# Weight requests in ScalarE's queue, behind the copy of the unit four back

## The chip, the core and the metric

The kernel runs on one core of a Trainium2 chip. The metric is the device time of one execution in microseconds (us). The core has TensorE (matrix products), VectorE, ScalarE, GpSimd and SyncE; each works through its own list of instructions in order and waits for the others by semaphores. Transfers between HBM and the on-chip memory are asked for by an instruction in some engine's list, here almost all in SyncE's, and are then carried by 16 DMA engines.

## The reference

Two layers over 256 tokens of width 2048, all in float32, and a final RMSNorm:

```
layer 0: hn = rmsnorm(x); proj = hn @ w_in            (2048 x 6656)
         mixer A: 8 query heads on 2 key/value heads, band of +-128 tokens, ALiBi, a sink
         mixer B: 8 heads, three dilated windows merged by their softmax denominators, ALiBi
         x = x + (concat(A, B) * silu(z)) @ w_out     (2048 x 2048)
layer 1: hn = rmsnorm(x); q, k, v, z = hn @ w_in      (2048 x 8192)
         mixer C: 16 heads, 2-D neighbourhood attention with a relative bias
         x = x + (C * silu(z)) @ w_out                (2048 x 2048)
out    = rmsnorm(x) * g
```

The weights are 296 units of 512 KB; activations stay on chip.

## The kernel before

**Products.** A float32 product is made of three products of rounded parts: weight and activation are each split into a rounded high part and the rest. The list `PLAN` gives the blocks of columns in order. `block_fm` makes a block of 128 columns (2 units), `block_tm` one of 512 or 256 (8 or 4 units). Layer 1 ends its projections with four gate blocks of 512 columns (kind `"z"`), called z0 to z3 here.

**A weight unit's way.** `load_unit` (L132) keeps up to `AHEAD` = 5 units asked for: for each it takes one of five buffers `raw`, and asks for the unit in SyncE's list (L136). `split` (L146) rounds it on ScalarE into one of three buffers `wh` (L149, "the copy"), and VectorE forms what is left in one of three buffers `wl` (L150, "the rest"). TensorE then uses both parts (L172 and L174 in `block_fm`, L205 in `block_tm`). A buffer `raw` is free once copy and rest of its unit are done, so the request of a unit waits for the rest of the unit five before it. While the first block is made, each request is followed by one for the piece of x that goes with it (`load_x`, L507); later requests carry the four loads of x by rows (L606).

**Beside the weights.** Attention and gates run between the blocks, each piece some blocks later (`later`, `tick`), or one piece after each split (`chores`). A transpose of a 256 x 256 matrix is a *turn*: VectorE transposes 32 x 32 blocks (L249), SyncE stores them in HBM (L251), and four loads bring them back (L258). `gate` evacuates a gate block by four activations on ScalarE (L464, L465, two each) and two operations on VectorE (L466), and then turns it. Bias tables are loaded in SyncE's list too (L498, L503). So SyncE's one list holds weights, turns and tables.

**Order.** The code is written block by block, and a gate's evacuation stands in it before the splits of the next block. The framework that builds the program sets the order of each engine's list when it builds, so the lists follow the code only roughly; on the chip each list is strictly in order.

The functions that the change touches:

Of the kernel before, what the change touches and what calls it, by code (L numbers as in the profile page):

```python
# [32 lines left out]
AHEAD = 5  # L33
# [51 lines left out]
NU = sum(n * D // (P * UNIT) for _, _, _, n, _ in PLAN)  # L85
# [18 lines left out]
def build(tc, ctx, xt, xr_in, wt, head, sink, rpb, tabs, gl_in, out):  # L104
    nc = tc.nc
# [23 lines left out]
    pos = [0]  # L129
    beside, chores, ahead = deque(), deque(), deque()  # L130

    def load_unit():  # L132

        while len(ahead) < AHEAD and pos[0] < NU:
            raw = wp.tile([P, UNIT], F32, name="raw", bufs=AHEAD)
            nc.sync.dma_start(raw, wt[pos[0]])  # L136
            k = pos[0] * UNIT // PLAN[0][3]
            if k < NK:
                load_x(k, k + UNIT // PLAN[0][3])
            elif beside:  # L140
                beside.popleft()()
            pos[0] += 1
            ahead.append(raw)
        return ahead.popleft()

    def split(raw):  # L146
        h = wp.tile([P, UNIT], F32R, name="wh")
        lo = wp.tile([P, UNIT], F32R, name="wl")
        nc.scalar.copy(h, raw)  # L149
        nc.vector.tensor_sub(lo, raw, h.bitcast(F32))  # L150
        if chores:
            chores.popleft()()
        return h, lo
# [11 lines left out]
    def block_fm(aa):  # L165

        ps = ps_p.tile([P, 2, S], F32, name="pp")
        per = UNIT // HD
        parts = [split(load_unit()) for _ in range(NK // per)]
        ks = [(k, k // per, slice(k % per * HD, (k % per + 1) * HD)) for k in range(NK)]  # L170
        for k, u, c in ks[:-1]:
            nc.tensor.matmul(ps, parts[u][0][:, c], aa[:, k], start=k == 0, stop=False)  # L172
        for k, u, c in ks:
            nc.tensor.matmul(ps[:, 0], parts[u][1][:, c], aa[:, k, 0], start=False, stop=False)  # L174
        k, u, c = ks[-1]
        nc.tensor.matmul(ps, parts[u][0][:, c], aa[:, k], start=False, stop=True)  # L176
        return ps
# [7 lines left out]
    def block_tm(n, aa, begin=False):  # L185

        pss = [ps_p.tile([P, n], F32, name="pp") for _ in range(NT)]
        per = UNIT // n
        for u in range(NK // per):
            if not begin:  # L190
                h, lo = split(load_unit())
            elif u == 0:
                h, lo = first_unit(n)
            else:
                h, lo = split(load_unit())
                for k in range(u * per, (u + 1) * per):
                    split_x(k, 0, x[:, k, :])
            for kk in range(per):
                k = u * per + kk
                c = slice(kk * n, (kk + 1) * n)  # L200
                todo = [(t, i) for t in range(NT) for i in range(3)]
                if begin and u == 0:
                    todo.sort(key=lambda e: e[1])
                for t, i in todo:
                    nc.tensor.matmul(pss[t], aa[:, k, i // 2, t * P:(t + 1) * P], (h, lo, h)[i][:, c],  # L205
                                     start=k == 0 and i == 0, stop=k == NK - 1 and i == 2)
            if u % 2 and u < NK // per - 1:
                tick()
        return pss
# [296 lines left out]
    def load_x(k0, k1):  # L506
        nc.sync.dma_start(x[:, k0:k1, :], xt[:, k0:k1, :])  # L507
# [221 lines left out]
```

## Time and profile before

| | |
|---|---|
| time, median of 3 runs | 889.69 us (887.34 to 892.37) |
| the profiled execution | 889.07 us, its span 887.3 us |
| TensorE busy | 868.3 us, 98% |
| VectorE busy | 599.0 us, 68% |
| ScalarE busy | 502.4 us, 57% |
| HBM read and written | 187.7 and 21.0 MB, 235 GB/s over the span |
| share of TensorE in the chain of waits that ended last | 94% |

Times in the profile count from the start of the span. PE is TensorE's multiplication and PEld its load of stationary operands, DVE is VectorE, ACT ScalarE, SP SyncE, and SPq its list of requests. In a timeline a row has the start, the duration, the engine, the line, the operation, what it writes and reads, and how many were merged; in brackets stands how long the engine had been idle before it, and what ended that. An instruction in `[...] <-X` waited for X last.

### The profile page before, as it was taken

What the parts mean: (1) busy time and instruction counts of PE and PEld (TensorE: products, weight loads), DVE (VectorE), ACT (ScalarE), POOL (GpSimd) and SP (SyncE); (2) the same over time, 40 slices, a digit from 0 to 9 for tenths busy, and PEclk for the clock granted to TensorE, in tenths of its full rate; (3) what the DMA queues carried; (4) which work ended last, traced back from release to release, by engine and by line L of the source; (5) the groups of instructions that cost most, each with busy time, mean ns of one, the idle gap of its engine ahead of it and who ended that gap; (6) DMA issues with size and microseconds to landing.
All of it is one profiled execution on the core that took longest, in us unless ns stands there. A gap on an engine that the chain in (4) does not pass through costs nothing.

```text
span 887.3 us, 12303 instructions
## 1 busy us (share of the span) xinstructions
PE 868.3 (98%) x4218; PEld 732.9 (83%) x4218; DVE 599.0 (68%) x972; ACT 502.4 (57%) x858; POOL 0.9 (0%) x7
## 2 busy tenths in 40 slices
PE   9999999999999999999999999999999998899995
PEld 7898888889888888888888888888888876688884
DVE  6576867788677766667556666766666666666563
ACT  7646666676556555555455565556555655454452
POOL 0000000000000000000000000000000000000000
PEclk9999999999999999999999999999999999999999
DMA  9868777779767677777677767786687578667642
GB/s 353 305 201 256 223 248 254 214 228 278 225 211 233 230 239 252 245 240 241 214 238 233 258 223 259 226 268 243 200 272 272 196 220 297 197 208 274 210 165 96
DMA packets 104607, 209.53 MB, mean 236 GB/s; under 512 B 11744, under 2 KB 52704, under 8 KB 104416
## 3 DMA queue, kind: packets, MB, share of 16 engines
q1 hardware_dynamic: 104544, 208.74, 71.7%
q8 instruction: 33, 0.54, 0.3%
q14 instruction: 30, 0.25, 0.1%
HBM read 187.72 MB, written 20.97 MB: 235 GB/s over the span
## 4 chain that ended last, share of the span: by engine, by line
PE 94%; ACT 2%; DVE 1%; DMA 1%; issue 1%; SPq 0%; ACTq 0%; DVEq 0%
PE pp L205 70%; PE pp L172 10%; PE pp L174 6%; PE pp L293 1%; PE pp L292 1%; PE pp L294 1%; PE pS L369 1%; PE pY L163 1%; PE pY L162 1%; PE pS L368 1%; PE pS L367 1%; PE pY L161 1%; DMA raw<-wt 1%; DMA y<-xt 1%; PE pp L176 1%; ACT wh L149 1%
## 5 line engine op out<-in xcount | busy, mean ns | idle before, releaser
L150 DVE TENSOR_TENSOR wl<-raw,wh 128x1024 fp32r<-128x1024 f32 x291 | 354.5, 1222 | 218.7 <-ACT wh L149 188.8
L205 PE MATMUL pp<-wh,xx 128*128 128x512 f32 (+1 forms) x1472 | 457.1, 387 | 6.3 <-ACT wh L149 6.0
L149 ACT CAST wh<-raw 128x1024 fp32r<-128x1024 f32 x291 | 305.0, 1052 | 255.2 <-PE pp L205 207.1
L205 PEld LDWEIGHTS pp<-wh,xx 128*128 128x128 f32 x1472 | 275.8, 189 | 62.0 <-ACT wh L149 7.0
L205 PE MATMUL pp<-wl,xx 128*128 128x512 f32 (+1 forms) x736 | 285.3, 388 | 2.7 <-DVE wl L150 2.7
L205 PEld LDWEIGHTS pp<-wl,xx 128*128 128x128 f32 x736 | 139.4, 189 | 31.3 <-DVE wl L150 4.9
L205 PE MATMUL pp<-wh,yy 128*128 128x512 f32 x448 | 138.4, 389 | 0.0
L205 PEld LDWEIGHTS pp<-wh,yy 128*128 128x128 f32 x448 | 84.1, 188 | 17.5
L172 PE MATMUL pp<-xx,wh 128*128 128x512 f32 x390 | 93.7, 392 | 0.0
L205 PE MATMUL pp<-wl,yy 128*128 128x512 f32 x224 | 87.1, 389 | 0.0
L172 PEld LDWEIGHTS pp<-xx,wh 128*128 128x128 f32 x390 | 72.1, 188 | 14.6
L174 PEld LDWEIGHTS pp<-xx,wl 128*128 128x128 f32 x416 | 53.3, 191 | 2.0
L174 PE MATMUL pp<-xx,wl 128*128 128x256 f32 x416 | 54.0, 283 | 0.0
L205 PEld LDWEIGHTS pp<-wl,yy 128*128 128x128 f32 x224 | 42.1, 188 | 8.6
L379 ACT ACTIVATE s<-s,nm 128x256 f32<-128x256 f32 x64 | 32.0, 501 | 12.1 <-DVE nm L374 10.2
L371 DVE SCALAR_TENSOR_TENSOR s<-pS,qs,tab 128x256 f32<-128x256 f32 x64 | 28.4, 475 | 5.1 <-PE pS L369 5.0
L249 DVE STREAM_TRANSPOSE tt<-p 128x256 f32<-128x256 f32 x64 | 26.2, 435 | 7.9 <-ACT p L388 7.9
L388 ACT ACTIVATE p<-s,rd 128x256 f32<-128x256 f32 x64 | 29.0, 501 | 4.3 <-DVE rd L385 4.2
L181 ACT COPY sum<-pp 128x256 f32<-128x256 f32 x26 | 9.6, 371 | 37.5 <-PE pp L176 37.4
L407 ACT CAST ph<-pT 128x256 fp32r<-128x256 f32 x64 | 23.3, 405 | 11.3 <-DMA pT<-bounce 11.3
L408 DVE TENSOR_TENSOR pl<-pT,ph 128x256 fp32r<-128x256 f32 x64 | 24.4, 418 | 6.1 <-ACT ph L407 6.0
L374 DVE TENSOR_REDUCE nm<-s 128x2 f32<-128x512 f32 x32 | 21.7, 679 | 0.2
(124 smaller groups left out, 582.5 us busy)
## 6 DMA issues: line engine op xcount, KB each, us to landing
raw<-wt SPq DMA_DIRECT2D x295, 512.0 KB, 4.5
bounce<-tt SPq DMA_DIRECT2D x56, 256.0 KB, 2.7
pT<-bounce SPq DMA_DIRECT2D x224, 64.0 KB, 3.3
tab<-tabs SPq DMA_DIRECT2D x32, 128.0 KB, 4.9
tab<-rpb SPq DMA_DIRECT2D x16, 256.0 KB, 4.1
pair<-tt SPq DMA_DIRECT2D x16, 256.0 KB, 3.0
ka<-pair SPq DMA_DIRECT2D x64, 64.0 KB, 4.0
xr<-xr SPq DMA_DIRECT2D x4, 512.0 KB, 5.2
```

The costliest lines, as they stand in the source:

```text
L149: nc.scalar.copy(h, raw)
L150: nc.vector.tensor_sub(lo, raw, h.bitcast(F32))
L172: nc.tensor.matmul(ps, parts[u][0][:, c], aa[:, k], start=k == 0, stop=False)
L174: nc.tensor.matmul(ps[:, 0], parts[u][1][:, c], aa[:, k, 0], start=False, stop=False)
L205: nc.tensor.matmul(pss[t], aa[:, k, i // 2, t * P:(t + 1) * P], (h, lo, h)[i][:, c], start=k == 0 and i == 0, stop=k == NK - 1 and i == 2)
L249: nc.vector.transpose(tt[:, :, :, t, :].rearrange("p b c i -> p c b i"), srcs[t])
L371: nc.vector.scalar_tensor_tensor(s[:, t, :], pS[:, t, :], R["qs"][:, t:t + 1], tab[:, t, :], op0=OP.mult, op1=OP.add)
L374: nc.vector.tensor_reduce(nm, s, axis=AX.X, op=OP.max, negate=True)
L379: nc.scalar.activation(s[:, t, :], s[:, t, :], AF.Exp, bias=nm[:, t:t + 1], accum_out=den[:, t:t + 1])
L388: nc.scalar.activation(p[:, t, ::step], s[:, t, :], AF.Copy, scale=rd[:, t:t + 1])
L407: nc.scalar.copy(dh, src)
L408: nc.vector.tensor_sub(dl, src, dh.bitcast(F32))
```

## The change

The request of a unit moves from `load_unit` into `split`. `load_unit` only asks by itself when nothing has been asked for, which happens once, at the first unit after the head: then it asks for five units in SyncE's list as before. After that, `split` asks for one unit behind each copy, in ScalarE's list, so that four are ahead at any time. In this order the request of unit u + 4 stands behind the copy of unit u; its buffer is that of unit u - 1, whose rest must be done. The loads of x that go with the requests, the turns and the tables stay in SyncE's list.

```diff
-    def load_unit():
-
-        while len(ahead) < AHEAD and pos[0] < NU:
+    def fetch(n, eng):
+
+        while len(ahead) < n and pos[0] < NU:
             raw = wp.tile([P, UNIT], F32, name="raw", bufs=AHEAD)
-            nc.sync.dma_start(raw, wt[pos[0]])
+            eng.dma_start(raw, wt[pos[0]])
             k = pos[0] * UNIT // PLAN[0][3]
...
             pos[0] += 1
             ahead.append(raw)
+
+    def load_unit():
+        if not ahead:
+            fetch(AHEAD, nc.sync)
         return ahead.popleft()
 
     def split(raw):
...
         nc.scalar.copy(h, raw)
+        fetch(AHEAD - 1, nc.scalar)
         nc.vector.tensor_sub(lo, raw, h.bitcast(F32))
```

## Rows read from the trace of the kernel before

**Rows 1.** The page: busy time of each engine, share of the span, instructions.
```profile
PE 868.3 (98%) x4218; PEld 732.9 (83%) x4218; DVE 599.0 (68%) x972; ACT 502.4 (57%) x858; POOL 0.9 (0%) x7
```
**Rows 2.** Stretches: us; PE, PEld, DVE, ACT, POOL busy; clock; DMA share; GB/s.
```profile
0.00:10.00 10.00, 8.57 (x34) 7.24 (x35) 4.72 (x9) 5.47 (x8) 0.93 (x7) 1.00 0.78 274
10.00:12.00 2.00, 2.00 (x11) 1.62 (x10) 1.53 (x3) 1.84 (x4) 0.00 (x0) 1.00 1.04 416
10.00:704.00 694.00, 694.00 (x3464) 590.76 (x3463) 481.85 (x789) 406.63 (x709) 0.00 (x0) 1.00 0.75 245
...
740.00:744.00 4.00, 4.00 (x12) 3.16 (x11) 3.08 (x6) 0.86 (x1) 0.00 (x0) 0.57 0.99 330
764.00:768.00 4.00, 1.25 (x3) 0.80 (x4) 3.93 (x7) 4.00 (x7) 0.00 (x0) 0.91 0.17 66
768.00:772.00 4.00, 4.00 (x13) 3.12 (x12) 2.70 (x5) 0.75 (x2) 0.00 (x0) 0.66 0.79 243
```
**Rows 3.** Waits of TensorE in 704 to 736: total us, times, longest.
```profile
PE pp L205 <- DVE wl L150: 0.9, 3, 0.4
PE pp L205 <- ACT wh L149: 0.4, 1, 0.4
```
**Rows 4.** Timeline of TensorE, 704 to 780, its long waits.
```profile
737.58 0.73 PE L205 MATMUL pp<-wh,xx 128*128 128x512 f32 x2 [2.77 <-ACT wh L149]
739.16 0.50 PE L205 MATMUL pp<-wl,xx 128*128 128x512 f32 x1 [0.85 <-DVE wl L150]
...
765.88 0.73 PE L205 MATMUL pp<-wh,xx 128*128 128x512 f32 x2 [2.77 <-ACT wh L149]
767.48 0.80 PE L205 MATMUL pp<-wl,xx 128*128 128x512 f32 x1 [0.87 <-DVE wl L150]
```
**Rows 5.** Timeline of SyncE's list, 690 to 780.
```profile
708.87 0.34 SPq L251 DMA_DIRECT2D bounce<-tt  x1
...
712.60 0.38 SPq L136 DMA_DIRECT2D raw<-wt  x1
...
748.54 0.93 SPq L136 DMA_DIRECT2D raw<-wt  x2
```
**Rows 6.** Timeline of VectorE, 690 to 780: two of its rests.
```profile
700.11 1.23 DVE L150 TENSOR_TENSOR wl<-raw,wh 128x1024 fp32r<-128x1024 f32 x1 [1.50 <-ACT wh L149]
...
712.90 2.32 DVE L150 TENSOR_TENSOR wl<-raw,wh 128x1024 fp32r<-128x1024 f32 x2
```
**Rows 7.** Timeline of ScalarE, 690 to 780: copies and gates.
```profile
704.84 1.05 ACT L149 CAST wh<-raw 128x1024 fp32r<-128x1024 f32 x1 [2.05 <-PE pp L205]
...
706.88 0.69 ACT L464 ACTIVATE s<-pp,rh 128x512 f32<-128x512 f32 x1
...
755.84 1.04 ACT L149 CAST wh<-raw 128x1024 fp32r<-128x1024 f32 x1
...
762.47 0.69 ACT L464 ACTIVATE s<-pp,rh 128x512 f32<-128x512 f32 x1 [3.22 <-PE pp L205]
...
764.77 2.01 ACT L149 CAST wh<-raw 128x1024 fp32r<-128x1024 f32 x2
```
**Rows 8.** The tile raw, whole span: requests (ns), and time to landing.
```profile
L136 SPq DMA_DIRECT2D raw<-wt x295: 327/333/2128, 1.6 to 858.6; - x148
...
DMA to landing us min/median/max: 3.1/4.5/8.8
```
**Rows 9.** Waits of SyncE's list, whole span: total us, times, longest.
```profile
SPq L251 <- DVE tt L249: 111.2, 47, 8.3
...
SPq L136 <- DMA raw<-wt: 14.3, 14, 2.6
```
**Rows 10.** Timeline of ScalarE, 20 to 30: the copies of unit 7 and unit 10.
```profile
20.33 1.05 ACT L149 CAST wh<-raw 128x1024 fp32r<-128x1024 f32 x1 [0.86 <-PE pp L205]
...
28.49 1.05 ACT L149 CAST wh<-raw 128x1024 fp32r<-128x1024 f32 x1 [1.67 <-PE pp L205]
```
**Rows 11.** Groups of ScalarE: the copies, busy us, mean ns, idle before them.
```profile
L149 ACT CAST wh<-raw 128x1024 fp32r<-128x1024 f32 x291 | 305.0, 1052 | 255.2 <-PE pp L205 207.1 <-DMA raw<-wt 19.7 <-DMA pT<-bounce 7.6
```

## The prediction

> **What bounds the kernel now.** I began with the busy shares: the reader sees TensorE busy in 98% of the span, VectorE in 68%, ScalarE in 57% [rows 1]. So only time in which TensorE waits, or runs at a lower clock, can be won. The table of stretches shows where that is: from 10 to 704 us it is busy in every microsecond [rows 2], and beside the start and the last 9 us all of it lies between 704 and 772 us, in the gate blocks of layer 1 (z0 to z3, eight weight units each). There the waits of TensorE give 0.9 and 0.4 us in 704 to 736 [rows 3], and its timeline a pair at the start of z2, 2.77 us for the copy of the first unit and 0.85 for its rest (the difference that VectorE forms), and a second such pair at z3, 2.77 and 0.87 us [rows 4]. That is 7.26 us in four waits. [...] All in all 1.3 + 7.26 + 3.4 = 12.0 us are open to this change.
>
> Why these waits stand there is in SyncE's queue and in ScalarE's order. The rest of z0's last unit is done at 701.34 [rows 6], which frees the buffer of z1's unit 4; its request goes out only at 712.60, 11.3 us later, since SyncE stood before a turn whose transposes weren't done until 708.87, with more loads behind that [rows 5]. TensorE didn't need the unit yet, but the units of z1 come late one after another, and with them the 1.3 us. At z2 and z3 the order is what holds. z0's gate (706.88) has two copies for z1 ahead of it, the last at 704.84, so TensorE goes on while ScalarE evacuates; z2's gate starts at 762.47 with no copy for z3 ahead of it (the one at 755.84 is of z2's own last unit), and z3's first two copies come at 764.77, behind four activations [rows 7]. Yet those units were asked for at 748.54 [rows 5], and a unit lands within 8.8 us [rows 8], so they were there by 758.3. In the code every gate stands before the next block's copies, so each engine's list isn't the code's order: it was fixed when the program was built, by when the builder thought an operand would be there. With weights behind turns and loads in one queue it thought them late.
>
> **The change, part by part.**
>
> *Requests leave SyncE.* Of 295 requests [rows 8] the first five stay (the first fetch), 290 move. SyncE saves 290 x 0.33 = 96 us of issuing, which no chain needs: worth nothing by itself. What counts is that a weight no longer stands behind a turn that waits (111.2 us in 47 waits, the longest 8.3 [rows 9], hidden under TensorE everywhere but here), and a turn no longer behind a weight's buffer. In z1 to z3 the request comes right behind the copy of the unit four back, some 10 us before now. Four units take 4 x (1.05 + 1.67) = 10.9 us [rows 10], the landing 8.8 at most, so no copy waits for its weights. That takes the 1.3 us. Whether it also puts the first copies ahead of the gates of z1 and z2 hangs on the order in which the new program is built: bounds 0 and 7.26 + 3.4 = 10.7 us. I take the whole, by the nearest row, z0's gate, where they stand ahead and TensorE doesn't stop. What is late next there is VectorE's rest behind the gate, some 0.2 us by my estimate, as part of the 0.9 is [rows 3].
>
> *Requests enter ScalarE's queue.* No row shows a request in it. Below: nothing, since the copy before it runs 1.05 us and an issue takes 0.33. Above: SyncE's spacing in a burst, 0.93 us for two [rows 5], so 290 x 0.46 = 133 us. ScalarE idles 255.2 us just before the copies [rows 11], and in the steady stretch 1.67 us of each 2.72 [rows 10]; either end is covered there. Without cover, behind a gate with three copies in a row, it is 2 x 0.46 us on the third. I take 1.0 us for the whole run, between 0 and 3. [...]
>
> *A wait is added on ScalarE.* The request needs the rest of the unit before the one just copied. In the steady stretch that is done: copy and rest take some 2.3 us of 2.72. In z1's start it isn't: the rests of two units run from 712.90 to 715.22 [rows 6], after both copies, so a request behind the second copy holds ScalarE until the first is done at 714.1, at least 1.2 us, and behind it stand casts, softmax and the next copies. TensorE doesn't notice up to 3.1 us: copy and rest take 2.3 us, and the buffers they write are free two units, 5.44 us, before TensorE needs them. SyncE's requests also waited 14.3 us in 14 pieces, the longest 2.6, for an earlier transfer to land [rows 9]; that stays below 3.1. I take 0 here; what lies above it is the slow rival.
>
> *The start.* Unit 6 and later come through a second queue while the first still holds units 4 and 5 with their x. Asked for by 10 us (sizes from the code): 0.8 for the head, 5 x 0.52 for units, 5 x 0.26 for x, 4.7 MB; landed 274 GB/s x 10 = 2.7; the 2.0 left take 4.8 us at 416 GB/s [rows 2], or 9.6 if shared evenly with units 6 to 8. Then x of unit 5 lands at 19.6 and its split ends at 20.5, and TensorE begins unit 5 at 20.33, when the copy of unit 7 gets unit 4's buffer [rows 10]. Bounds 0 and 2 us, I take 0.5. The rows of x that SyncE may now load early (2 MB) stand behind these in its queue, so not before about 22 us.
>
> Sum, against the profiled execution (889.07 us, span 887.3 and 1.8 around it): -12.0 + 0.2 + 1.0 + 0.5 = -10.3, so 878.8. The median of the runs shown is 0.6 above that execution; I say 879.4.
>
> **The rivals.**
> R1, the order stays: the weights land early, but the gate's four activations still stand before the copies at z2 and z3. Then only the 1.3 us go, and 1.0 + 0.5 come: 889.3. For it: at z3 the weights were there and the order alone held TensorE. Against: the builder put them right at z0. Between lies that one of the two goes: 889.07 - 1.3 - 5.3 + 1.7 = 884.2.
>
> R2, the slower side: ScalarE is held at a request for over 3.1 us, in the stages with turns (30 to 320, 475 to 700), by a rest on VectorE that lags or by an earlier transfer which itself stands in SyncE behind a turn (up to 8.3 us [rows 9]); copies and evacuations behind it come late and TensorE runs dry. One such event costs what a pair costs, 3.6 + 1.7 = 5.3 us. With both z pairs gone it decides from the second event on; three give 878.8 + 16 = 894.8, and with the pairs still there a single one gives 889.3 + 5.3 = 894.6. For it: a queue in which nothing waited for a turn would be tied to one. Against: in 694 us there is no wait of TensorE at all now, so the slack is nowhere used up.
>
> R3, nothing moves: the transfers themselves are late, not their requests, since the same transfer engines carry both queues; then 889.1. For it: 416 GB/s at the start [rows 2], where they are all busy. Against: z3's first units were asked for 16 us before their copy. [...]
>
> **How the numbers follow.** Forecast (both pairs go) 0.42, with its own range of 877 to 882; one of the two goes 0.13; R1 0.17; R2 0.20; R3 0.08. Faster by over 0.5% (4.4 us, about what a measurement of this kernel tells from no change) means below 885.2: 0.55, the first two. Slower means above 894.1: 0.17 of R2's 0.20, as its mildest form ends below. Same: 0.28. The low end is all 12.0 us gone and nothing paid, 877.0; the high end is R2 in either form, 894.8, so 895.
>
> **What would show it.** Right: no wait of TensorE at the starts of z2 and z3, two copies ahead of each gate in ScalarE's timeline, a clock of 1.00 through 736 to 772, and ScalarE's requests some 10 us before the copies they serve. Wrong: copies still behind the gates (R1); waits of TensorE for copies inside 30 to 700 with a request ahead of them on ScalarE (R2); copies waiting for weights that were asked for in time (R3); or waits for x of over 2 us in all before 22 us.

## The result, and the profile after

The changed kernel takes 946.25 us (median of 6 runs, 944.90 to 955.89) against 889.34 before. The ratio of the means is 1.066, with a 95% interval of 1.061 to 1.071; one run of before, of 4205 us, is left out of it. The kernel is 57 us slower, where 879.4 and a range up to 895 were forecast.

The profiled execution of the changed kernel is its longest, 955.89 us with a span of 954.1 and a mean granted clock of 0.983, where the four shortest took 944.9 to 946.7 us at 0.992 to 0.994, so sums from its rows come out some 10 us too high. Its lines after L136 stand four to five lower than before: the copy is L153 (was L149), the rest L155 (L150), `block_tm` L210 (L205), a turn's store L256 and its loads L263 (L251, L258), the gate's activations L469 and L470 (L464, L465).

The page of after: busy shares, transfer queues, and the chain that ended last.

```profile
PE 898.6 (94%) x4218; PEld 736.2 (77%) x4218; DVE 595.4 (62%) x972; ACT 499.5 (52%) x858; POOL 0.9 (0%) x7
...
q10 hardware_dynamic: 41760, 152.06, 48.2%
q1 hardware_dynamic: 62784, 56.68, 19.3%
...
PE 62%; DMA 18%; DVE 9%; ACT 5%; SPq 3%; issue 2%; ACTq 0%; DVEq 0%
```

VectorE and ScalarE do what they did [rows 1]; TensorE's share falls from 98 to 94%. The weights' 152 MB now go through a queue of their own, q10. TensorE held 94% of the chain before; now transfers, VectorE and ScalarE make up a third of it. Of the 66.8 us by which the span grew, 36.5 are idle time of TensorE (954.1 - 898.6 less 887.3 - 868.3). The mean granted clock fell from 0.994 to 0.983 over the span; that is 10.9 us by estimate (0.017 x 954.1 less 0.006 x 887.3), and about what this execution took beyond the median, so the clock has next to no part in the 57 us. The other 19 are in longer busy time, the cause of which no view shows.

Stretches of after, with the columns of [rows 2]: the start, the stretch of layer 0 with turns, its end and the next projections, the attention of layer 1, and the rest.

```profile
0.00:100.00 100.00, 93.14 (x475) 78.32 (x476) 60.60 (x109) 56.46 (x100) 0.92 (x7) 0.98 0.70 243
100.00:320.00 220.00, 205.30 (x1081) 172.44 (x1080) 146.80 (x259) 121.03 (x238) 0.00 (x0) 0.98 0.67 209
320.00:475.00 155.00, 149.33 (x660) 119.53 (x659) 98.46 (x166) 76.99 (x119) 0.00 (x0) 0.99 0.68 220
475.00:704.00 229.00, 222.34 (x1011) 181.36 (x1010) 139.76 (x210) 120.51 (x205) 0.00 (x0) 0.99 0.73 236
704.00:954.10 250.10, 228.48 (x1000) 184.56 (x998) 149.81 (x233) 124.55 (x198) 0.00 (x0) 0.97 0.63 205
```

Where TensorE never stopped before (10 to 704 us [rows 2]) it now idles in every stretch. So the loss isn't at the gates z0 to z3 alone, on which the forecast was spent. The waits of TensorE over the whole span say for what (total us, times, longest), first before, then after:

```profile
PE pp L205 <- ACT wh L149: 6.0, 3, 2.8
PE pp L205 <- DVE wl L150: 2.7, 5, 0.9
...
PE pp L210 <- DVE wl L155: 29.5, 27, 3.8
PE pp L210 <- ACT wh L153: 5.0, 8, 1.0
PE pp L177 <- ACT wh L153: 3.7, 6, 1.2
```

It waits for split weights: 38.2 us for copies and rests, against 8.7 in all before. Yet the weights themselves are there. The views of ScalarE in after put 9.3 us, in 5 waits of its copies, down to a transfer of weights, where [rows 11] had 19.7 in all; and at four of the five the unit had landed over 5 us before its copy began, so that only the first, 1.17 us at 7.59, is a wait for weights. What stands ahead of the copies is shown by one place in ScalarE's timeline of after:

```profile
123.60 1.05 ACT L153 CAST wh<-raw 128x1024 fp32r<-128x1024 f32 x1 [0.96 <-DMA raw<-wt]
128.48 0.34 ACTq L136 DMA_DIRECT2D raw<-wt  x1
129.00 0.41 ACT L412 CAST ph<-pT 128x256 fp32r<-128x256 f32 x1 [4.35 <-DMA pT<-bounce]
...
129.62 2.00 ACT L153 CAST wh<-raw 128x1024 fp32r<-128x1024 f32 x2
```

and by the same place of before (the third pair of casts of turned softmax there, L407):

```profile
113.74 1.06 ACT L149 CAST wh<-raw 128x1024 fp32r<-128x1024 f32 x1 [0.87 <-PE pp L205]
114.72 0.71 ACT L407 CAST ph<-pT 128x256 fp32r<-128x256 f32 x2
```

Before, 39 copies stand ahead of this cast and it finds its operand there. After, only 37 do, and ScalarE idles 4.35 us until the turn has landed; two copies come behind it, and TensorE waits 0.39 us for the rest of the first (131.98). This place alone doesn't tell the cast from the request ahead of it, which went out only at 128.48; the experiments do. The chain of after from 98 to 132 us shows two turns in a row on the path that sets the end (start, us, what):

```profile
99.00 3.82 DMA bounce<-tt
...
104.40 5.02 DMA pT<-bounce
109.54 0.76 DVE y L488 x2
110.31 1.15 DVE wl L155
111.50 3.26 PE pp L210 x13
...
119.20 4.55 DMA bounce<-tt
...
125.10 3.83 DMA pT<-bounce
129.00 0.46 ACT ph L412 x2
129.62 1.05 ACT wh L153
130.70 1.24 DVE wl L155
131.98 5.29 PE pp L210 x22
```

From the start of its store to the end of its loads a turn takes some 10 us; an addition of VectorE or a cast of ScalarE waits for them, and a rest or copy for TensorE waits behind that.

The turns are slower, too. The pages of before (the first two lines) and after have, of transfers by line, KB each and the median us to landing:

```profile
bounce<-tt SPq DMA_DIRECT2D x56, 256.0 KB, 2.7
pT<-bounce SPq DMA_DIRECT2D x224, 64.0 KB, 3.3
...
raw<-wt ACTq DMA_DIRECT2D x290, 512.0 KB, 4.4
bounce<-tt SPq DMA_DIRECT2D x56, 256.0 KB, 4.2
pT<-bounce SPq DMA_DIRECT2D x224, 64.0 KB, 4.3
```

and the waits of SyncE's list, before and after, for its loads behind their store:

```profile
SPq L258 <- DMA bounce<-tt: 31.9, 36, 3.8
...
SPq L263 <- DMA bounce<-tt: 130.4, 45, 5.7
```

The lists themselves, compared instruction by instruction in the built programs (the shift is the mean over all places):

```
places that differ    ScalarE      VectorE      TensorE
after / before        611 of 768   812 of 970   1891 of 4205
mean shift            2.1          2.6          4.1 places
```

On ScalarE, what consumes a turn stands on average 1.4 copies earlier in after, and the activations of softmax 2.2.

### The profile page after: what moved, and what is told of

Read it like the earlier page. It is cut to its first block, busy times and chain, and to the rows that moved or that the text cites. A ratio compares the mean times of both kernels' runs of the same rounds, so it can differ in the third digit from the quotient of the medians.

```text
span 954.1 us, 12128 instructions
## 1 busy us (share of the span) xinstructions
PE 898.6 (94%) x4218; PEld 736.2 (77%) x4218; DVE 595.4 (62%) x972; ACT 499.5 (52%) x858; POOL 0.9 (0%) x7
## 4 chain that ended last, share of the span: by engine, by line
PE 62%; DMA 18%; DVE 9%; ACT 5%; SPq 3%; issue 2%; ACTq 0%; DVEq 0%
PE pp L210 45%; DMA pT<-bounce 8%; PE pp L177 6%; DMA bounce<-tt 5%; PE pp L179 4%; DVE wl L155 4%; SPq L263 2%; DMA raw<-wt 2%; ACT wh L153 2%; DVE tt L254 1%; DMA pair<-tt 1%; DVE s L376 1%; DVE s L471 1%; DMA ka<-pair 1%; DMA sk<-sink 1%
## 5 line engine op out<-in xcount | busy, mean ns | idle before, releaser
L210 PE MATMUL pp<-wh,xx 128*128 128x512 f32 (+1 forms) x1472 | 463.8, 393 | 7.3 <-ACT wh L153 4.7
L155 DVE TENSOR_TENSOR wl<-raw,wh 128x1024 fp32r<-128x1024 f32 x291 | 351.6, 1219 | 108.5 <-ACT wh L153 107.2
L153 ACT CAST wh<-raw 128x1024 fp32r<-128x1024 f32 x291 | 301.8, 1049 | 119.4 <-PE pp L210 73.0
L210 PEld LDWEIGHTS pp<-wh,xx 128*128 128x128 f32 x1472 | 277.0, 192 | 64.5 <-ACT wh L153 8.2
L210 PE MATMUL pp<-wl,xx 128*128 128x512 f32 (+1 forms) x736 | 292.6, 398 | 24.4 <-DVE wl L155 24.1
L210 PEld LDWEIGHTS pp<-wl,xx 128*128 128x128 f32 x736 | 141.4, 192 | 64.8 <-DVE wl L155 37.0
L210 PE MATMUL pp<-wh,yy 128*128 128x512 f32 x448 | 140.7, 393 | 0.4 <-ACT wh L153 0.3
L177 PE MATMUL pp<-xx,wh 128*128 128x512 f32 x390 | 97.2, 394 | 3.9 <-ACT wh L153 3.7
L210 PEld LDWEIGHTS pp<-wh,yy 128*128 128x128 f32 x448 | 84.6, 190 | 18.9 <-ACT wh L153 1.7
L210 PE MATMUL pp<-wl,yy 128*128 128x512 f32 x224 | 89.1, 398 | 5.5 <-DVE wl L155 5.4
L210 PEld LDWEIGHTS pp<-wl,yy 128*128 128x128 f32 x224 | 42.4, 189 | 18.7 <-DVE wl L155 10.1
L412 ACT CAST ph<-pT 128x256 fp32r<-128x256 f32 x64 | 23.1, 406 | 39.0 <-DMA pT<-bounce 27.1
L488 DVE TENSOR_TENSOR y<-y,pT 128x256 f32<-128x256 f32 x22 | 8.5, 422 | 29.0 <-DMA pT<-bounce 23.3
```

What stands on the lines that cost most here:

```text
L412: nc.scalar.copy(dh, src)
```

## The experiments

Theories: **hold** (R2: ScalarE stands at a request, and what is behind it is late), **order** (the builder laid other lists, and copies stand behind waits for turns), **rings** (weights in a second queue make the transfers of turns slower). Before took 889.3 to 889.5 us in each set of runs; intervals are of the ratio to it.

**1. Hold alone.** The bulk of each unit goes through SyncE again; the last 8 columns, 4 KB, are asked for by ScalarE at the changed place, behind the same buffers.

```diff
-            eng.dma_start(raw, wt[pos[0]])
+            if eng is nc.scalar:
+                nc.sync.dma_start(raw[:, :UNIT - 8], wt[pos[0]][:, :UNIT - 8])
+                nc.scalar.dma_start(raw[:, UNIT - 8:], wt[pos[0]][:, UNIT - 8:])
+            else:
+                nc.sync.dma_start(raw, wt[pos[0]])
```

> Weights go back to SyncE's list, all but the last 8 of 1024 columns of each unit (4 KB), which ScalarE asks for where the change put the whole request; so both lists keep a request per unit, and ScalarE's has the same waits as in the changed kernel. Theory order (the builder sees SyncE's list nearly empty, thinks turns quick, and lists their consumers ahead of the copies, which then wait for the turn): 885 to 900 us, as SyncE's list is as full as before. Theory rings (turns take longer because weights come through a second queue beside them): 885 to 900, as the weights are back in the turns' queue. Theory hold (ScalarE is held at its requests by VectorE's rests and by earlier transfers): 930 to 950.

Measured: 887.42 us, 0.998 [0.997, 0.999]. 290 requests on ScalarE, most of them with a wait, cost nothing. The lists of ScalarE, VectorE and TensorE differ from before's in 152, 197 and 156 places only, by 0.2 to 0.3 on average. The run speaks for short holds alone: in its timeline ScalarE stands idle until a request goes out for 79.6 us in all, never over 1.9 at once, while after has as much in all, 79.3 us, but twelve pieces beyond the start of 2 to 4 us.

**2. The mirror.** ScalarE asks for 1016 columns, SyncE for the last 8.

> The mirror of the run before: ScalarE asks for 1016 of 1024 columns of each unit, SyncE for the last 8 at the same place of the code. Theory order: 885 to 905, SyncE's list has a request for each unit again. Theory rings: 940 to 955, the bulk still comes through the second queue. Theory hold: 940 to 955, ScalarE waits for the same as in the changed kernel.

Measured: 945.18 us, 1.062 [1.059, 1.065], like after. I expected SyncE's list, full of requests again, to bring before's order back. It didn't: the lists differ in 609, 813 and 1833 places. Between these two kernels the order went with the long transfers, not with the number of requests. So this run does not tell order from rings; it only shows that the bytes, and not the number of requests in a queue, carry the loss.

**3. Another engine asks.** The same requests in GpSimd's list, which has nothing else to do.

```diff
-        fetch(AHEAD - 1, nc.scalar)
+        fetch(AHEAD - 1, nc.gpsimd)
```

> The requests of the change are made by GpSimd, which has nothing else to do, instead of ScalarE; SyncE's list is as empty as in the changed kernel. Theory hold: 880 to 900, as no engine with work is held. Theories order and rings: 935 to 955, since SyncE's list is empty and the weights come through a queue of their own.

Measured: 934.76 us (923.54 to 943.79), 1.047 [1.039, 1.054]. Here no request can hold ScalarE, and 41 us (by the ratio) to 45 (by the median) are still lost. What the rest of the 57 are isn't told by this run, nor does it put a price on the hold: its lists are others again (310, 364 and 127 places off before's, 627, 796 and 1919 off after's).

**4. Three ahead.** The request then needs the rest of the unit two before the copy, which is long done.

```diff
-        fetch(AHEAD - 1, nc.scalar)
+        fetch(AHEAD - 2, nc.scalar)
```

> The changed kernel with three units ahead instead of four in the same five buffers, so that a request behind a copy needs the rest of the unit two before, not one before. Theory hold, if it is the rests that hold ScalarE: below 925. Theories order and rings: 940 to 965, the lead of three units (8.2 us) is hardly more than the longest landing (8.3), so it may be worse than the change.

Measured: 954.62 us, 1.076 [1.071, 1.080]. A wait for VectorE's rest is not what costs: the waits of ScalarE that its view puts down to a rest fall from 43.9 us in after to 3.6, with lists that differ from after's in 4, 6 and 0 places, and nothing is gained.

**5. The new place alone.** The request behind the copy and four ahead, but in SyncE's list.

```diff
-        fetch(AHEAD - 1, nc.scalar)
+        fetch(AHEAD - 1, nc.sync)
```

> The requests stand where the change puts them, behind the copy of the unit four back, but in SyncE's list. Theories order and rings: 885 to 895, since it is the second queue that does the harm and not the place or the lead of four. If the lead of four were too short: 930 and more.

Measured: 889.11 us, 1.000 [0.999, 1.001]. ScalarE's, VectorE's and TensorE's lists are those of before, without a difference. So place and lead cost nothing; the queue does.

**6 and 7. Order and queue, each alone.** At the end of the build, every instruction of ScalarE, VectorE and TensorE (requests for transfers excepted) is tied behind the one that should precede it, by a dependency that orders the list and adds no semaphore. Before, tied to its own lists, builds into the same program, so the ties themselves change nothing. SyncE's list is left to the builder, and without the weights it is 231 and 224 of 431 places off before's in the two kernels, so each difference below has some of SyncE's order in it. One kernel is after with before's three lists, the other before with after's three lists.

```diff
         tick()
+    pin(tc)
...
+        for a, b in zip(seq, seq[1:]):
+            tc.add_manual_dep(b, a.name, info, reason="order")
```

> The changed kernel, weights asked for by ScalarE, but the lists of ScalarE, VectorE and TensorE (requests aside) are tied to the order that they have in the kernel before, by order-only dependencies that make nothing wait on the chip. Theory order (the lost time comes from lists in which consumers of turns stand earlier): 878 to 895 us. Theory rings (turns take longer on the chip beside the second queue): 930 to 950, as the weights still come through it. Theory hold is out already.

> The mirror: the kernel before, weights asked for by SyncE, with the three lists tied to the order of the changed kernel. Theory order: 925 to 960, or more, as turns stand behind weights again. Theory rings: 885 to 900.

Measured: 904.01 us, 1.016 [1.015, 1.018], for after with before's lists, and 927.21, 1.043 [1.039, 1.047], for before with after's lists. The four kernels make a table:

```
weights asked for in    before's lists   after's lists   by the lists
SyncE's queue           889.4            927.2           37.8
ScalarE's queue         904.0            946.3           42.3
by the queue            14.6             19.1
```

So two thirds of the loss or more go with the lists, whichever queue the weights are in; and with the weights in SyncE's queue no request stands in ScalarE's list to hold it. After's lists make TensorE wait for rests even with one queue. From the views of waits, TensorE in before with after's lists:

```profile
PE pp L205 <- DVE wl L150: 17.9, 21, 2.9
PE pp L205 <- ACT wh L149: 4.3, 4, 2.4
```

and in after with before's lists:

```profile
PE pp L210 <- ACT wh L153: 8.1, 4, 2.8
PE pp L210 <- DVE wl L155: 7.8, 7, 2.9
```

Of the 15.9 us in the latter, 7.25 are before's two pairs at z2 and z3 [rows 4]. Two more waits, 1.42 us at 301.28 and 2.34 at 316.03, follow casts at which ScalarE stands for a turn, with no request going out in between:

```profile
298.48 0.41 ACT L412 CAST ph<-pT 128x256 fp32r<-128x256 f32 x1 [4.24 <-DMA pT<-bounce]
...
312.35 0.41 ACT L412 CAST ph<-pT 128x256 fp32r<-128x256 f32 x1 [6.67 <-DMA pT<-bounce]
```

The waits of ScalarE and of SyncE's list over the whole span show the slow turns as well:

```profile
ACT ph L412 <- DMA pT<-bounce: 65.2, 24, 6.7
...
SPq L263 <- DMA bounce<-tt: 155.7, 47, 6.5
```

Its page has 4.1 us for a store and 4.4 for a load. Before, that cast waited 11.3 us in 7 pieces, and the loads 31.9 in 36. With after's lists and one queue, the page has 3.4 and 3.2.

**8 and 9. What slows the turns.** Both with before's lists. First, ScalarE asks for 1016 columns and SyncE for 8, so that SyncE's list keeps the pace of the weights; second, each unit comes by two requests of 512 columns, so its rows are half as long.

```diff
+                nc.scalar.dma_start(raw[:, :UNIT - 8], wt[pos[0]][:, :UNIT - 8])
+                nc.sync.dma_start(raw[:, UNIT - 8:], wt[pos[0]][:, UNIT - 8:])
...
+                eng.dma_start(raw[:, :UNIT // 2], wt[pos[0]][:, :UNIT // 2])
+                eng.dma_start(raw[:, UNIT // 2:], wt[pos[0]][:, UNIT // 2:])
```

> The lists of the kernel before, ScalarE asks for 1016 of 1024 columns of each unit and SyncE for the last 8. If the 15 us that stayed with the lists of before tied come from the weights' bytes in a second queue: 898 to 912. If they come from SyncE's list running ahead without requests that wait for buffers: 886 to 895.

> The lists of the kernel before, the whole weights asked for by ScalarE, each unit in two requests of 512 columns, so with rows of 2 KB instead of 4 KB. If turns lose on the transfer engines because their short rows take turns with the weights' long ones: pT<-bounce lands in under 4.0 us (4.4 with the long rows) and the time is 892 to 901. If not: 4.3 or more and 900 to 915.

Measured: 913.71 us, 1.027 [1.024, 1.031], and 917.33, 1.030 [1.028, 1.032]. The first says that SyncE's list running ahead of the weights isn't the cause, since tied to their pace again it loses more; a store takes 4.1 us and a load 4.0 there. The second is inconclusive: loads land in 3.8 us, stores in 4.3, and the time isn't lower, so the length of a weight's rows isn't shown to be what matters; its view of ScalarE also puts 50.8 us of waits of copies down to weights, where after with before's lists has 7.1. What goes on between two queues on the 16 transfer engines stays open, but the traces narrow it. A store that is asked for while no unit is under way (asked for and not yet landed) lands in 2.0 to 2.1 us (medians) in before, in after, and in after with before's lists; there are 17 such stores of 56 before, and 6 and 4 in the other two. Asked for beside one unit, a store takes 3.0, 4.0 and 3.8 us. So stores meet a weight more often, and land later beside one. In before with after's lists, in one queue, a store beside one unit takes 3.7 us, so landing later isn't the second queue's alone.

**10. Only where the gain was seen.** Requests in ScalarE's queue from z0 on, in SyncE's before that.

```diff
+        if pos[0] >= IZ:
+            fetch(AHEAD - 1, nc.scalar)
```

> ScalarE asks for weights only from the first unit of z0 on; all earlier ones are asked for by SyncE, five ahead, as in the kernel before. Forecast's reason (in the gate blocks SyncE's queue holds weights back): 877 to 886, the two pairs of waits gone. Theories order and rings: the part after 684 us, 23% of the time, loses like the whole, about 15 us, so 895 to 908.

Measured: 890.28 us, 1.002 [1.000, 1.003]. Waits of TensorE from 700 to 780 us in it:

```profile
PE pp L212 <- DVE wl L157: 6.7, 6, 2.7
PE pp L212 <- ACT wh L154: 0.8, 1, 0.8
```

The pairs of [rows 4] began with a wait for a copy, 2.77 us each; those are gone, but rests are late in their place. The builder's new order isn't the wanted one here either.

**11 and 12. The wanted order, written out.** Before with its own lists tied, but for this: the first two copies and rests of z2 and of z3 stand ahead of the gates of z1 and z2. Weights in SyncE's queue in one kernel, in ScalarE's from z0 on in the other.

> The kernel before, weights in SyncE's list, with its own lists tied except that the first two copies of z2 and of z3, and their rests, stand ahead of the gate of the block before. If the order alone holds the two pairs of waits: 877 to 883 us, 10.7 us less at most (7.3 of waits, 3.4 of clock). If the weights are too late there for lack of an early request: 886 to 895, the copies then keep the gate waiting.

> The same lists, and ScalarE asks for the weights from z0 on. If SyncE's queue held the weights back in the gate blocks: 874 to 882, below the run before by the 1.3 us of small waits and more. If the second queue costs there what it costs over the whole kernel (some 15 us in all, 3 to 4 in this quarter): 881 to 890, above the run before.

Measured: **877.80 us, 0.986 [0.984, 0.988]**, with every request in SyncE's list, in before's order: 1.4% faster than before, and the lowest time here. With ScalarE asking from z0 on, 880.60 us, 0.989 [0.987, 0.991], an interval that meets the other. Two stretches of the faster one, with the columns of [rows 2]:

```profile
736.00:744.00 8.00, 7.40 (x31) 5.84 (x32) 7.80 (x14) 5.73 (x13) 0.00 (x0) 1.00 0.82 263
764.00:772.00 8.00, 8.00 (x39) 6.73 (x39) 4.15 (x5) 3.43 (x4) 0.00 (x0) 1.00 1.00 309
```

ScalarE's timeline of it, before and at the gates of z1 and z2:

```profile
733.72 1.05 ACT L149 CAST wh<-raw 128x1024 fp32r<-128x1024 f32 x1 [0.26 <-DMA raw<-wt]
735.05 1.05 ACT L149 CAST wh<-raw 128x1024 fp32r<-128x1024 f32 x1 [0.28 <-PE pp L205]
736.00 0.68 ACT L464 ACTIVATE s<-pp,rh 128x512 f32<-128x512 f32 x1
...
756.58 1.06 ACT L149 CAST wh<-raw 128x1024 fp32r<-128x1024 f32 x1 [0.27 <-ACT wh L149]
758.58 0.69 ACT L464 ACTIVATE s<-pp,rh 128x512 f32<-128x512 f32 x1 [0.94 <-PE pp L205]
```

The waits of its TensorE for split weights, whole span:

```profile
PE pp L205 <- DVE wl L150: 2.1, 5, 0.5
...
PE pp L205 <- ACT wh L149: 0.2, 1, 0.2
```

Copies stand ahead of each gate, TensorE waits 2.3 us for split weights in the whole span, and the granted clock is 1.00 where it was 0.57 and 0.66 [rows 2].

## Why the prediction was wrong, point by point

**The step that failed** is in the part on leaving SyncE: the order in which the new program is built. It was priced at two places, as a gain between 0 and 10.7 us, and taken at the gain. The premise was right: lists are fixed when the program is built, by when the builder thinks an operand will be there. But the same premise holds for every list over the whole span. With weights in a queue of their own the lists were built with what consumes a turn 1.4 copies further ahead, and on the chip the turns don't come that early (its casts of turned softmax wait 27.1 us for loads in after, 11.3 before); that the builder thought they would is an inference. These lists cost 38 to 42 us, shown by exchanging them with the queue unchanged (6 and 7). "The order changes" had a rival in which it stays, and none in which it gets worse elsewhere.

**Rival R3 and the second queue.** The forecast gave a late transfer the price of nothing moving, 889.1, with a chance of 0.08; by it a second queue gains nothing and costs nothing. That both queues use the same transfer engines is in after's trace: of the time of 16 engines, q1 alone takes 101.9% from 8 to 9 us, q10 alone 94.8% from 53 to 54, and the two side by side 52.5 and 50.9% from 19.5 to 20.5. The profiles of these runs also bear out that the second queue brings no transfer forward (a unit lands in 4.4 us at the median, 4.5 before), but not that it costs nothing: with the three lists held fixed, the second queue takes 14.6 us on before's lists and 19.1 on after's, with stores of turns at 4.1 us for 2.7. That a turn might get slower was in no term of the sum. It is shown to come with the weights' bytes in the other queue (8); how, is shown only as far as stores meet a weight more often there.

**R2** had the right sign and a wrong mechanism. It asked for ScalarE held at a request for over 3.1 us. Before with after's lists has no request in ScalarE's list and loses 37.8 us (7); three units ahead, with hardly a wait for rests left, gains nothing (4). Holds aren't absent in after: of the twelve pieces of 2 to 4 us named in experiment 1, three are over 3.1. What these cost isn't separated; it is within the 14.6 to 19.1 us by the queue. Nor is every wait that is put down to a weight's transfer a hold: the view of ScalarE's waits puts 18.8 us, in five pieces, of instructions that read no weight (softmax, casts of turns and of heads, squares) down to a transfer of a weight, but in the timeline the last request ahead of each had gone out 2.9 to 4.6 us before. The remark against R2, that the slack is nowhere used up in 694 us, was true of before's lists alone, and a stretch without a wait doesn't tell how much slack is left.

**The term for issuing** (1.0 us, between 0 and 3) holds: 334 ns each at the median in the view of the tile raw, and 887.42 us in experiment 1, not above before. The lower bound is seen too: in after's timeline a request goes out at 30.56 us, while ScalarE's copy ahead of it runs from 30.50 to 31.55.

**The weights are there in time**: right. Units land in a median of 4.4 us, and of the five waits put down to a transfer only the 1.17 us of the first unit, which SyncE asks for, is a copy waiting for its own.

**The start** was put at 0.5 us between 0 and 2. TensorE's timeline of after has one wait for x just above that:

```profile
21.23 0.80 PE L210 MATMUL pp<-wh,xx 128*128 128x512 f32 x1 [2.35 <-DVE xx L162]
```

With before's lists the waits for x come to 0.9 us, and in before with after's lists to 5.3, so most of it is order as well.

**The 12.0 us open at the gates**: right in size and cause, and credited to the wrong edit. Two copies and their rests moved ahead of each of two gates gain 11.7 us (889.5 to 877.8) with every request where it was. No run shows the 3.4 us for the clock in that sum apart from the waits, nor the 1.7 for one pair; they are an estimate from the clocks of [rows 2], 0.43 x 4 after z2's pair and 0.09 x 4 + 0.34 x 4 after z3's. What before's trace shows is a granted clock of 0.50 from 740 to 743 us and of 1.00 from 744 to 748, and three products of `block_tm` every 1.28 us in the first and every 0.70 in the second:

```profile
741.19 1.05 PE L205 MATMUL pp<-wh,xx 128*128 128x512 f32 x2
742.04 0.63 PE L205 MATMUL pp<-wl,xx 128*128 128x512 f32 x1
742.47 1.05 PE L205 MATMUL pp<-wh,xx 128*128 128x512 f32 x2
...
744.29 0.62 PE L205 MATMUL pp<-wh,xx 128*128 128x512 f32 x2
744.75 0.39 PE L205 MATMUL pp<-wl,xx 128*128 128x512 f32 x1
744.99 0.61 PE L205 MATMUL pp<-wh,xx 128*128 128x512 f32 x2
```

The change itself doesn't get them: after waits 11.7 us for rests between 740 and 860 us, in 7 pieces. And 0.42 for both pairs going rested on one gate, z0, where the builder had happened to choose well.

## What to carry to other kernels

When a framework lays the lists, moving a transfer to another engine's queue can be an edit of every list, and its price has to be read over the whole span, not where the gain is hoped for; compare the built lists, and tie the old order to see what is left of the change. Where a trace shows an operand present and its consumer behind something else, move the consumer: two copies moved ahead of each of two gates won what no other queue did. Small transfers that a chain waits for should not be assumed as fast beside bulk traffic of a second queue as behind it in one: on the same lists, stores of 256 KB took 4.1 us for 2.7 here and loads of 64 KB 4.4 for 3.3.

## What the runs showed of the hardware

A request in ScalarE's list takes 334 ns of that list at the median in after; in experiment 1, 290 of them, for 4 KB each, take nothing of the kernel's time (887.42 us, 889.29 before). In GpSimd's list one took 530 ns.

With the weights in the second queue, a 256 KB store and 64 KB loads of the first one took 4.2 and 4.3 us for 2.7 and 3.3, at a lower mean traffic (219 GB/s over the span, 235 before). The mean hides that 50 of the 56 stores were asked for while a unit was under way, 39 before. With before's lists, at half the rows' length the loads took 3.8 us and the stores 4.3, and the time rose from 904.0 to 917.3 us.
